# Layer 1 of a two-layer hybrid block: adaLN dots taken out of the input projection, a retention norm set behind two attention heads, and every move between partitions on the gpsimd queue

## The chip, the cores and the metric

One core of one Trainium2 chip runs the whole program. The metric is device time of one launch in microseconds (us), as the median of several runs. Below, PE is the matrix engine (TensorE), DVE the vector engine, ACT the scalar engine, POOL the gpsimd engine, and SP the sync engine, which does nothing here but issue DMAs. Each engine takes its instructions one after another in the order in which the program was written to its queue, and waits at an instruction until the data it needs is there.

## What is computed

Two layers, each with a token mix and an MLP, over 512 latent tokens and 256 context tokens of width 1024. The parts that matter here are cut from the reference:

```python
mod_x = (jax.nn.silu(c) @ w_ada[l] + b_ada[l])[:, None, :]       # 6 x 1024 numbers per layer
sh1, sc1, g1, sh2, sc2, g2 = jnp.split(mod_x, 6, axis=-1)
hx = modulate(rmsnorm(x, norm_mix[l]), sh1, sc1)
...
rq_l, rk_l, rv_l, rg_l, cq_l, ckv_l, kpe_l, u_l = split_proj(hx @ w_in)
...
ret_l = retention_out(o_rl, rg_l)          # 4 retention heads, head norm, gate
mla_l = blocked_attend(qn_l, qp_l, kn_all, kpe_all, v_all)      # 8 heads of 96
pool_l = pool_branch(u_l, w_pool, pool_scale)
out_l = jnp.concatenate([ret_l, mla_l, pool_l], axis=-1) @ w_out
x = x + g1 * ox
x = x + g2 * sq_relu_mlp(modulate(rmsnorm(x, norm_mlp[l]), sh2, sc2), w_ff1[l], w_ff2[l])
```

Twelve pieces of 512 numbers make up the adaLN vector of a layer. The first four (shift and scale of the mix) are needed at the layer's start; pieces 4 and 5 (g1) at the end of its token mix, 6 to 9 (shift and scale of the MLP) after it, 10 and 11 (g2) inside the MLP.

## The kernel before, in words

All activations stand transposed, features on partitions and tokens along the free axis. Every fp32 matmul is done as three fp32r matmuls (`mm3`), a high and a low part of each operand. So each weight tile that DMA brings into a buffer `raw` is split: ACT copies the high part (line 228) and DVE subtracts to get the low part (line 237), both into a tile `wt`. Weight and row loads are all issued by SP (line 253).

**adaLN as dots.** For layer 1 the adaLN vector isn't computed by matmuls but on DVE: one *dot* loads a 128x512 piece of `w_adaT` (256 KB) into a buffer `rows`, of which there are three (`N_RR`), and one `scalar_tensor_tensor` with an accumulating output (line 492) multiplies it by the broadcast silu(c) and sums. Eight dots make one of the twelve pieces, followed by two small adds (lines 499 and 500). A buffer is loaded again only when its dot has been done.

**Tasks, streams and the order on the queues.** The program is a list of tasks with costs. `merge` interleaves several lists in proportion to their costs. `layer_mix` builds the token mix of a layer as: rk and rq (retention keys and queries) first; then a merge of the values `rv_tok` and the other input projections with the dots of the key "in"; then a merge of the two retention pairs (`ret_pair`, ordered by `lagged`) with q, k and v of the first heads and the dots of "ret"; then eight attention heads in two halves, `att[0:4]` merged with the dots of "att" and `att[4:8]` with those of "att2". After that comes the MLP, whose first up projections are merged with the dots of "ff1". Which pieces belong to which key stands in the table `where` in `build`; those named in none are done in the MLP of layer 0. The framework then settles the final order of each engine's queue from these tasks, and it may place an instruction that is free early ahead of others; the order on the queues, not that of the list, is what the engines follow.

**Names.** `rv` is the result of `rv_tok` for one of six tiles of 128 tokens, in one of four PSUM buffers; ACT copies 32 columns of it out (`kp`, line 753), DVE takes the head means (`mu`, lines 756 and 757) and writes `V` (line 758), which releases the PSUM buffer. So the fifth tile, rv4, can begin only when V of rv0 has been written, and rv5 when V of rv1 has. `A` is the result of a projection: u0, u1 (pooling), ckv, cq0, cq1. `sc` are attention scores, DVE takes their row maximum (`st`, line 1033), ACT exponentiates (`p`, line 1034), PE transposes (`pT`) and multiplies with v (`pv`, `po`).

**Moves between partitions.** Head and rope parts of q and k have to change partition, which a DMA from SBUF to SBUF does (`move`, line 234). Layer 1 has 64 of them: 16 for `KS`, 16 for `QQ` and 8 for each of four pairs of heads (`q<-rope`, `q<-q`, `k<-k`, `k<-kpT`). A counter sends them to gpsimd and SP in turn, 32 each (`MV`, line 74).

Of the kernel before, what the change touches and what calls it, by code (L numbers as in the profile page):

```python
# [73 lines left out]
MV = lambda k, i: (i + 1) % 2  # L74
# [70 lines left out]
def merge(*streams):  # L145

    total = [max(sum(t.cost for t in s), 1e-9) for s in streams]
    done = [0.0] * len(streams)
    at = [0] * len(streams)
    out = []  # L150
    while True:
        live = [i for i in range(len(streams)) if at[i] < len(streams[i])]
        if not live:
            return out
        i = min(live, key=lambda j: (done[j] + 0.5 * streams[j][at[j]].cost) / total[j])
        t = streams[i][at[i]]
        at[i] += 1
        done[i] += t.cost
        out.append(t)


class Net:
# [67 lines left out]
    def move(self, out, src, kind):  # L230

        self.nm_ = getattr(self, "nm_", 0) + 1
        q = MV(kind, self.nm_)
        (self.nc.gpsimd, self.nc.sync, self.nc.scalar)[q].dma_start(out.bitcast(F32), src.bitcast(F32))

    def lo(self, out, src, hi):
# [440 lines left out]
    def layer_mix(self, l, late):  # L677
# [111 lines left out]
        def sig(i):  # L789
                t, e = self.tmp("sig")[:, :qw], self.tmp("sig")[:, :qw]  # L790
                nc.vector.tensor_scalar(t, s["rg"][:, i, :qw], -40.0, None, op0=ALU.max)
                nc.scalar.activation(e, t, AF.Exp, scale=-1.0)
                nc.scalar.activation(t, e, AF.Ln, bias=self.one)
                nc.scalar.activation(e, t, AF.Exp, scale=-1.0)
                nc.vector.tensor_tensor(s["rg"][:, i, :qw], s["rg"][:, i, :qw], e, op=ALU.mult)
# [188 lines left out]
        def q_pair(p):  # L984
            u, off = 1 + p // 2, 256 * (p % 2)
            t = s["q", 2 * p] = self.d("q")
            for o, n in qg:
                ps = self.B([P, n], "q")
                self.lin1(ps, mu[u], CQ, 2, o, n, woff=off)
                self.hi(t[:, 0, o:o + n], ps, scale=QK_SCALE)  # L990
                nc.vector.scalar_tensor_tensor(t[:, 1, o:o + n], ps, QK_SCALE, t[:, 0, o:o + n].bitcast(F32),
                                               op0=ALU.mult, op1=ALU.subtract)
            q = s["q", 2 * p + 1] = self.d("q")
            self.move(q[0:64, :, :qw], t[64:128, :, :qw], "q")
            for h in (2 * p + 1, 2 * p):
                for j in range(2):
                    self.move(s["q", h][64 + 16 * j:80 + 16 * j, :, :qw], s["qr"][j][16 * h:16 * h + 16, :, :qw], "qr")

        def k_pair(p):
            t = s["k", 2 * p] = self.d("k")  # L1000
            for o, n in ALL:
                ps = self.B([P, n], "k")
                self.lin1(ps, mu[1], CKV, 1, o, n, woff=512 + P * p)
                self.hi(t[:, 0, o:o + n], ps)
                self.lo(t[:, 1, o:o + n], ps, t[:, 0, o:o + n])
            k = s["k", 2 * p + 1] = self.d("k")
            self.move(k[0:64], t[64:128], "k")
            self.move(k[64:96], s["kpT"][0:32], "kr")
            self.move(t[64:96], s["kpT"][0:32], "kr")

        def v_quad(g, tk):
            ps = self.B([P, 256], "v")
            w = mu[2]
            x = CKV(0)[:, :, tk * P:(tk + 1) * P]
            c = slice(512 + 256 * g, 768 + 256 * g)
            self.mm3(ps, x[:, 0], x[:, 1], w[:, 0, c], w[:, 1, c], True, True)
            if tk == 0:
                s["v", g] = self.d("v", F32, (P, NT, 4, 64))
            nc.scalar.activation(s["v", g][:, tk], ps.rearrange("p (h e) -> p h e", h=4), AF.Copy)
# [184 lines left out]
        else:  # L1204
            early, mid, late = self.early
# [5 lines left out]
            early = [t for e in early for t in (behind[1], e, behind[0])]  # L1211
# [14 lines left out]
        if not l:  # L1226
# [12 lines left out]
        kv = lambda p: [Task(qc, lambda: q_pair(p), (mu[1 + p // 2],)),  # L1239
                        Task(kc, lambda: k_pair(p), (mu[1],))]  # L1240
        vq = lambda g: [Task(330, lambda tk=tk: v_quad(g, tk), (mu[2],)) for tk in range(NT)]
# [4 lines left out]
            J[n] = keys[2 + i]  # L1246
        j = lambda names: [J[n] for n in names.split()]
        ex = [self.extra.pop((n, l), []) for n in ("in", "ret", "att", "att2")]
        def lagged(n, sg):
            r = sum(ret, [])  # L1250
            i = len(ret[0]) - 1
            fin = r.pop(i)
            i = min(i + n, len(r) - 1)
            r.insert(i, fin)
            r.insert(max(len(r) - 1 - sg, 0), Task(0, lambda: sig(1)))
            r.insert(min(sg, i), Task(0, lambda: sig(0)))
            return r

        po, uq = pre[:2], pre[2:3]
        out = first[:n_first] + merge(first[n_first:] + (j('u1 u0 F KX ckv cq0 kn E cq1 rg0 SX qn K0 K1 SL ST rg1 uq') if l == 0 else j('u0 u1 ckv kpe KX cq0 kn cq1 F rg0 qn E SX K0 K1 SL ST rg1')), ex[0]) + merge(lagged(LG[l], SG[l]), (po + kv(0) + vq(0) if l == 0 else uq + kv(0) + vq(0)), ex[1])  # L1260
        att = att_tasks()
        sp = [Task(0, lambda n=n, i=i, at=at: mix_split(n, i, at)) for n, at in (("ret", 0), ("pool", 6)) for i in range(2)]
        early = sp + [Task(self.lin_cost(4, qg), lambda m=m: out_early(m), (out_units[m // 2],)) for m in range(NK)]
        out += (merge(merge(sum(att[0:2], []), kv(1) + vq(1)) + merge(sum(att[2:4], []), kv(2) + kv(3)), ex[2]) + merge(sum(att[4:8], [])[:-1], early, ex[3]) + att[7][-1:] if l == 0 else merge(merge(sum(att[0:2], []), kv(1) + po[:1] + vq(1) + po[1:] + kv(2)) + merge(sum(att[2:4], []), kv(3)), ex[2]) + merge(sum(att[4:8], [])[:-1], early, ex[3]) + att[7][-1:])
        out.append(Task(0, lambda: self.psum(0, 8)))
        return out

# [333 lines left out]
    def build(self):  # L1601
        nc, a = self.nc, self.a
        self.extra = {}
        self.gated = []
        self.mark = None
        tasks, late = [], []
        self.setup()
        LC = [(0, NL, 0), (NL, NC, 1)]

        def start(i):  # L1610
            if i == 0:
                self.stat_start()
            for k in (2 * i, 2 * i + 1):
                self.stat_push(k, 0, T)

        def begin():
            self.ahead, self.after = True, self.rows

        self.x_tiles(T)
        for i in range(4):  # L1620
            nc.sync.dma_start(self.x[i], a["xT"][:, 2 * i:2 * i + 2, :])
        first = [Task(0, lambda i=i: start(i)) for i in range(4)]
        ada = [self.ada_tasks(0, (n,), True) for n in range(4)]
        nl, ncx = self.norm_tasks(0, self.G1, 0, LC)
        zipped = sum(([a, b] for a, b in zip(first, ada[2])), [])
        tasks += first + nl[:2] + ncx[:1] + ada[2] + ada[0] + [Task(0, begin)]
        self.early = (ada[1] + ada[3], nl[2:6] + ncx[1:5], nl[6:] + ncx[5:])
        where = [dict(inv=(10,), att=(4,), ret=(5, 7), att2v=(6, 8, 9), ff1v=()),
                 dict(inv=(4,), attv=(5, 6), att2v=(7, 8, 9), ff1v=(10, 11))]
        for i in range(DEPTH):  # L1630
            for nme, cs in where[i].items():
                rows = nme[-1] == "v"
                ts = (self.ada_rows_tasks if rows else self.ada_tasks)(i, cs)
                key = nme[:-1] if rows else nme, i
                self.extra[key] = merge(self.extra.get(key, []), ts)
        rest = [n for n in range(12) if n not in sum(where[1].values(), ())]
        self.extra["ff", 0] = self.ada_rows_tasks(1, rest)
        gate = self.ada_rows_tasks(0, (11,))
        self.extra["out", 0] = merge(self.extra.get(("out", 0), []), gate[:4])
        self.extra["ff1", 0] = merge(self.extra.get(("ff1", 0), []), gate[4:])  # L1640
        sr = [Task(0, self.silu_rows), Task(0, self.decays)]
        self.sr = sr
        for l in range(DEPTH):
            tasks += self.extra.pop(("pre", l), [])
            tasks += self.layer_mix(l, late)
            out, late, whole, groups = self.layer_out(l)
            tasks += merge(out, self.extra.pop(("out", l), []))
            ff, late = self.layer_ff(l, whole, groups, late)
            tasks += ff

        self.emit(tasks + late)
        self.ps.close()
# [121 lines left out]
```

## Time and profile before

| | |
|---|---|
| median of 3 runs | 1567.8 us (1564.02 to 1570.93) |
| the profiled execution | 1565.01 us, of which the span of the profile is 1562.9 us |
| mean granted clock of PE | 0.992 of full speed |
| busy share of the span | PE 96%, DVE 76%, ACT 51%, POOL 2% |

The span is the time from the first to the last instruction of one execution, and about 2 us lie around it. Times within the profile are microseconds from the start of that span. Layer 0 fills the first 900 us of it. The token mix of layer 1 begins at about 909 us, its last input projections at 968 us, its attention at about 1050 us, and the MLP of layer 1 at 1205 us.

### The profile page before, as it was taken

How to read it: one execution, taken by the hardware profiler on the slowest of the kernel's cores; microseconds unless marked ns; L12 is line 12 of the kernel's file. 1: busy time of each engine (PE TensorE's matmuls, PEld its weight loads, DVE VectorE, ACT ScalarE, POOL GpSimd, SP SyncE). 2: the span in 40 equal slices, each digit the busy share in tenths (PEclk: the TensorE clock that was granted, in tenths of full speed). 3: DMA queues.
4: the chain of work that ended last, by engine and by line, in shares of the span. 5: the costliest groups of instructions: out<-in, count | busy, mean ns of one | idle time of the engine just before them, and what ended most of it. 6: DMA issues, size and time to landing. Idle time of an engine off the chain costs nothing.

```text
span 1562.9 us, 24541 instructions
## 1 busy us (share of the span) xinstructions
PE 1506.0 (96%) x9120; PEld 1329.2 (85%) x9120; DVE 1190.1 (76%) x2633; ACT 797.0 (51%) x1635; POOL 37.9 (2%) x78
## 2 busy tenths in 40 slices
PE   5999999999999999999999999989999999999997
PEld 2798667888899999999999998757888898989886
DVE  6668765887997887878869696997647895968844
ACT  4425467653654344344443463566655655455443
POOL 0110001000000000000000002001000000000000
PEclk9999999999999999999999999999999999999999
DMA  9463454555132413322223227547433443242321
GB/s 359 136 186 101 133 137 95 173 180 187 48 108 89 129 49 106 100 68 90 75 75 114 81 96 230 177 125 189 152 97 113 155 120 97 82 127 72 126 81 54
DMA packets 68903, 191.98 MB, mean 123 GB/s; under 512 B 8752, under 2 KB 11312, under 8 KB 68784
## 3 DMA queue, kind: packets, MB, share of 16 engines
q1 hardware_dynamic: 65440, 180.18, 36.6%
q0 software_dynamic: 2816, 9.70, 2.7%
q8 instruction: 72, 1.18, 0.3%
q10 hardware_dynamic: 528, 0.52, 0.1%
q14 instruction: 47, 0.39, 0.1%
HBM read 159.97 MB, written 10.49 MB: 109 GB/s over the span
## 4 chain that ended last, share of the span: by engine, by line
PE 83%; DVE 9%; ACT 3%; DMA 3%; issue 1%; SPq 0%; DVEq 0%; ACTq 0%
PE f L220 49%; PE A L220 9%; PE sc L220 4%; PE oe L220 3%; PE res L220 3%; PE pv L220 3%; PE rv L220 2%; PE pT L1052 2%; DMA rows<-w_adaT 2%; PE ada L220 1%; DVE wt L237 1%; DVE hn L572 1%; DVE h L576 1%; DVE rows L492 1%; PE ro L220 1%
## 5 line engine op out<-in xcount | busy, mean ns | idle before, releaser
L220 PE MATMUL f<-h,wt 128*128 128x384 f32 (+2 forms) x2400 | 454.3, 351 | 4.2 <-ACT h L575 3.5
L220 PEld LDWEIGHTS f<-h,wt 128*128 128x128 f32 x2400 | 416.8, 189 | 38.6 <-ACT h L575 4.5
L220 PE MATMUL f<-act,wt 128*128 128x256 f32 (+2 forms) x2664 | 410.0, 315 | 1.0 <-ACT wt L228 0.7
L220 PEld LDWEIGHTS f<-act,wt 128*128 128x128 f32 x2664 | 394.0, 188 | 15.7 <-ACT wt L228 3.5
L237 DVE TENSOR_TENSOR wt<-raw,wt 128x512 fp32r<-128x512 f32 x326 | 222.6, 687 | 101.2 <-ACT wt L228 99.9
L228 ACT ACTIVATE wt<-raw 128x512 fp32r<-128x512 f32 x326 | 198.7, 626 | 166.9 <-PE f L220 67.4
L220 PE MATMUL A<-h,wt 128*128 128x512 f32 (+1 forms) x912 | 172.9, 347 | 3.4 <-ACT h L575 2.4
L220 PEld LDWEIGHTS A<-h,wt 128*128 128x128 f32 x912 | 142.8, 190 | 29.5 <-ACT h L575 3.1
L228 ACT ACTIVATE wt<-sum 128x512 fp32r<-128x512 f32 x104 | 62.7, 629 | 126.8 <-DVE sum L264 103.4
L1437 ACT ACTIVATE b<-f 128x384 f32<-128x384 f32 (+3 forms) x100 | 50.6, 510 | 139.4 <-PE f L220 139.2
L492 DVE SCALAR_TENSOR_TENSOR rows<-rows,sbc 128x512 f32<-128x512 f32 x136 | 92.0, 685 | 8.1 <-DMA rows<-w_adaT 7.5
L220 PE MATMUL sc<-k,q 96*128 96x512 f32 (+1 forms) x384 | 87.2, 356 | 8.4 <-ACT p L1034 7.4
L220 PEld LDWEIGHTS sc<-k,q 96*128 96x128 f32 x384 | 64.4, 193 | 26.3 <-ACT p L1034 10.3
L237 DVE TENSOR_TENSOR wt<-sum,wt 128x512 fp32r<-128x512 f32 x104 | 70.3, 686 | 8.3 <-ACT wt L228 7.0
L1033 DVE TENSOR_REDUCE st<-sc 128x1 f32<-128x768 f32 x64 | 60.8, 952 | 13.7 <-PE sc L220 13.1
L1481 DVE SCALAR_TENSOR_TENSOR x<-f,mod,x 128x256 f32<-128x256 f32 (+2 forms) x148 | 69.6, 502 | 0.5 <-ACT V L1489 0.4
L1053 ACT ACTIVATE pT<-pT 128x384 f32<-128x384 f32 x128 | 56.8, 492 | 23.5 <-PE pT L1052 22.8
L228 ACT ACTIVATE act<-T 128x384 fp32r<-128x384 f32 (+1 forms) x104 | 47.3, 473 | 40.5 <-DVE T L1392 28.0
L1391 DVE TENSOR_TENSOR V<-V,f 128x384 f32<-128x384 f32 (+1 forms) x136 | 66.2, 513 | 0.1
L1034 ACT ACTIVATE p<-sc,st 128x768 f32<-128x768 f32 x64 | 57.9, 905 | 14.5 <-DVE st L1033 13.4
L220 PE MATMUL oe<-mix,wt 128*128 128x512 f32 (+1 forms) x288 | 60.8, 363 | 0.0
L237 DVE TENSOR_TENSOR act<-b,act 128x384 fp32r<-128x384 f32 (+2 forms) x94 | 47.4, 514 | 16.9 <-ACT act L228 16.9
(244 smaller groups left out, 1837.9 us busy)
## 6 DMA issues: line engine op xcount, KB each, us to landing
raw<-w_ff SPq DMA_DIRECT2D x128, 512.0 KB, 3.7
rows<-w_adaT SPq DMA_DIRECT2D x136, 256.0 KB, 3.2
raw<-w_in SPq DMA_DIRECT2D x22, 512.0 KB, 4.2
raw<-w_ada SPq DMA_DIRECT2D x16, 512.0 KB, 10.1
raw<-w_out SPq DMA_DIRECT2D x16, 512.0 KB, 4.2
rows<-w_ada SPq DMA_DIRECT2D x24, 256.0 KB, 3.1
x<-xd SPq DMA_DIRECT2D x6, 768.0 KB, 8.1
x<-xT SPq DMA_DIRECT2D x4, 768.0 KB, 6.5
```

The source lines that it names most:

```text
L220: return self.nc.tensor.matmul(out, l, r, start=start, stop=stop)
L228: self.nc.scalar.activation(out, src, AF.Copy, **k)
L237: return self.nc.vector.tensor_tensor(out, src, hi.bitcast(F32), op=ALU.subtract)
L492: nc.vector.scalar_tensor_tensor(out, w, 1.0, self.sbc[:, v, half], op0=ALU.mult, op1=ALU.mult, accum_out=acc[:, v, i, j:j + 1])
L572: nc.vector.scalar_tensor_tensor(t[:, :n], self.X(k)[:, o:o + n], G, self.ss[:, 1, o:o + n], op0=ALU.mult, op1=ALU.mult)
L1033: nc.vector.tensor_reduce(st[:, 0:1], ps, axis=AX, op=ALU.max, negate=True)
L1034: nc.scalar.activation(p, ps, AF.Exp, bias=st[:, 0:1], accum_out=st[:, 1:2])
L1052: nc.tensor.transpose(ps[:, kt, :], p[:, (k0 + kt) * P:(k0 + kt + 1) * P], self.ident)
L1053: nc.scalar.activation(s["pT", h, qt // 2][:, k0:k0 + 3, c], ps, AF.Copy)
L1391: add = lambda x, y, z, op=ALU.add: nc.vector.tensor_tensor(x, y, z, op=op)
L1437: nc.scalar.activation(b[:, at:at + n], ps, AF.Relu)
L1481: self.mark = nc.vector.scalar_tensor_tensor(x, ps[:, at - o:at - o + n], g[:, cond:cond + 1], x, op0=ALU.mult, op1=ALU.add)
```

## The change

Three things change, all for layer 1 alone.

1. `move` sends every move of layer 1 to gpsimd (queue 0) instead of alternately to gpsimd and SP.
2. The last two tasks of the second retention pair (the sigmoid of the gate, `sig(1)`, and the norm `fin_b`) are taken out of the retention stage, kept in `held`, and merged with the attention heads 2 and 3. The dots of "att" are merged with this second part only, heads 0 and 1 run without, and q and k of the third pair move to the first part.
3. Piece 4 moves from "in" to "att", piece 6 from "att" to "att2": "in" gets no dots (8 before), "att" 16 as before, "att2" 32 (24 before). The total remains.

```diff
@@ move
-        q = MV(kind, self.nm_)
+        q = 0 if self.layer else MV(kind, self.nm_)
@@ layer_mix
+        held = []
         def lagged(n, sg):
...
-            r.insert(max(len(r) - 1 - sg, 0), Task(0, lambda: sig(1)))
+            if l:
+                held.extend([Task(0, lambda: sig(1)), r.pop()])
+            else:
+                r.insert(max(len(r) - 1 - sg, 0), Task(0, lambda: sig(1)))
...
-   merge(merge(sum(att[0:2], []), kv(1) + po[:1] + vq(1) + po[1:] + kv(2)) + merge(sum(att[2:4], []), kv(3)), ex[2]) + ...
+   merge(sum(att[0:2], []), kv(1) + po[:1] + vq(1) + po[1:] + kv(2)) + merge(merge(sum(att[2:4], []), held + kv(3)), ex[2]) + ...
@@ build
-                 dict(inv=(4,), attv=(5, 6), att2v=(7, 8, 9), ff1v=(10, 11))]
+                 dict(attv=(4, 5), att2v=(6, 7, 8, 9), ff1v=(10, 11))]
...
+            tasks.append(Task(0, lambda l=l: setattr(self, "layer", l)))
```

What this does to the queues is seen only in the order of the instructions. The first difference on DVE is at the values rv of layer 1. In the kernel before, DVE's queue has there, after the third dot of layer 1, the means and V of one rv tile after another, and no dot until all six are done:

```order
L756 TENSOR_REDUCE mu_9949<-rv_9921 128x4
L757 TENSOR_SCALAR mu_9949<-mu_9949 128x4
L237 TENSOR_TENSOR rope_9883<-rm_9878,rope_9883 128x512
L756 TENSOR_REDUCE mu_9983<-rv_9957 128x4
L757 TENSOR_SCALAR mu_9983<-mu_9983 128x4
L758 TENSOR_TENSOR V_9946<-rv_9921,mu_9949 128x256
L758 TENSOR_TENSOR V_9946<-rv_9957,mu_9983 128x256
```

In the changed kernel 24 dots stand between the mean of rv0 and V of rv0. This is the beginning of that stretch, on DVE's queue again (`rows_…` is the buffer load of one dot):

```order
L756 TENSOR_REDUCE mu_9945<-rv_9917 128x4
L492 SCALAR_TENSOR_TENSOR rows_11153,acc_11151<-rows_11153,sbc 128x512
L237 TENSOR_TENSOR rope_9871<-rm_9866,rope_9871 128x512
L237 TENSOR_TENSOR rope_9879<-rm_9874,rope_9879 128x512
L757 TENSOR_SCALAR mu_9945<-mu_9945 128x4
L492 SCALAR_TENSOR_TENSOR rows_11180,acc_11151<-rows_11180,sbc 128x512
L756 TENSOR_REDUCE mu_9975<-rv_9949 128x4
L492 SCALAR_TENSOR_TENSOR rows_11183,acc_11151<-rows_11183,sbc 128x512
L757 TENSOR_SCALAR mu_9975<-mu_9975 128x4
L492 SCALAR_TENSOR_TENSOR rows_11208,acc_11151<-rows_11208,sbc 128x512
```

And this is its end, still on DVE's queue, with the first two V; the low half of u1's first weight (`wt_10099`) stands behind the fourteenth dot of the layer, and five more dots stand between V of rv1 and V of rv4:

```order
L492 SCALAR_TENSOR_TENSOR rows_11656,acc_11686<-rows_11656,sbc 128x512
L492 SCALAR_TENSOR_TENSOR rows_11661,acc_11686<-rows_11661,sbc 128x512
L758 TENSOR_TENSOR V_9942<-rv_9917,mu_9945 128x256
L758 TENSOR_TENSOR V_9942<-rv_9949,mu_9975 128x256
L756 TENSOR_REDUCE mu_10005<-rv_9979 128x4
```

Counted over DVE's queue, the 48 dots of pieces 4 to 9 stand as follows in the changed kernel: 3 ahead of the means of rv, 24 between the mean and V of rv0, 5 from there to V of rv4, 16 from there to the first row maximum of the attention (line 1033), and none inside the attention. In the kernel before: 3 ahead of the means, none among rv, 23 from there to the first row maximum, and 22 inside the attention. The 16 dots of pieces 10 and 11 in the MLP stay where they were.

On SP's queue the moves `KS` and `QQ` stood between the weights of the input projection in the kernel before:

```order
L253 DMA raw_9804<-w_in 128x1024
L234 DMA KS_9776<-rope_9771 32x768 x4
L234 DMA KS_9777<-rope_9771 32x768 x4
L253 DMA raw_9836<-w_in 128x1024
L253 DMA raw_9841<-w_in 128x1024
L234 DMA QQ_9886<-rope_9883 32x2x512 x2
L234 DMA QQ_9887<-rope_9883 32x2x512 x2
```

In the changed kernel the same stretch of SP's queue holds loads alone, and of the 17 from the fifth of these on 16 are loads of rows:

```order
L253 DMA raw_9800<-w_in 128x1024
L253 DMA raw_9832<-w_in 128x1024
L253 DMA raw_9837<-w_in 128x1024
L253 DMA raw_9915<-w_in 128x1024
L253 DMA rows_11153<-w_adaT 128x512
L253 DMA rows_11180<-w_adaT 128x512
L253 DMA rows_11183<-w_adaT 128x512
L253 DMA raw_10105<-w_in 128x1024
```

On PE's queue the kernel before turns after the first nine matmuls of u0 (`A_10128`) to rv4 (`rv_10050`), then does rv5, the rest of u0, u1 and ckv:

```order
L220 MATMUL A_10128<-h_1608_9316,wt_9913 128x512 x3
L220 MATMUL A_10128<-h_1609_9317,wt_9913 128x512 x3
L220 MATMUL A_10128<-h_1610_9318,wt_9913 128x512 x3
L220 MATMUL rv_10050<-wt_9796,h_1608_9316 128x288 x3
L220 MATMUL rv_10050<-wt_9796,h_1609_9317 128x288 x3
```

In the changed kernel PE does u0 and u1 whole after rv3, 24 matmuls each; here is the end of u1 (`A_10164`) and the beginning of rv4 (`rv_10039`), and behind rv5 follows ckv:

```order
L220 MATMUL A_10164<-h_1613_9321,wt_10102 128x512 x3
L220 MATMUL A_10164<-h_1614_9322,wt_10102 128x512 x3
L220 MATMUL A_10164<-h_1615_9323,wt_10102 128x512 x3
L220 MATMUL rv_10039<-wt_9792,h_1608_9316 128x288 x3
L220 MATMUL rv_10039<-wt_9792,h_1609_9317 128x288 x3
```

So rv4, which waits for V of rv0, has moved behind u1 on PE, and V of rv0 has moved behind 24 dots on DVE. On POOL's queue the 16 moves of `KS` and the 16 of `QQ` now stand in a row, and behind them the 32 moves of the pairs of heads.

## Rows read from the trace of the kernel before

**Rows 1.** The page, parts 1 and 4: busy shares, and the chain that ended last by engine.

```profile
PE 1506.0 (96%) x9120; PEld 1329.2 (85%) x9120; DVE 1190.1 (76%) x2633; ACT 797.0 (51%) x1635; POOL 37.9 (2%) x78
...
PE 83%; DVE 9%; ACT 3%; DMA 3%; issue 1%; SPq 0%; DVEq 0%; ACTq 0%
```

**Rows 2.** Windows: us, busy of PE, PEld, DVE, ACT, POOL, PEclk, DMA, GB/s.

```profile
1040.00:1080.00 40.00, 35.09 (x202) 27.73 (x200) 33.26 (x81) 27.50 (x62) 3.20 (x6) 0.91 0.65 183
1080.00:1120.00 40.00, 37.01 (x238) 29.66 (x237) 29.24 (x72) 26.97 (x61) 2.62 (x5) 0.96 0.66 173
```

**Rows 3.** Waits of PE, 940 to 1110 us: total us, times, longest.

```profile
PE sc L220 <- ACT p L1034: 6.3, 2, 3.3
PE ro L220 <- DVE P L882: 2.4, 1, 2.4
PE sc L220 <- issue: 1.1, 1, 1.1
```

**Rows 4.** Windows around the two falls of PE's clock; columns as in rows 2.

```profile
1053.60:1060.50 6.90, 5.55 (x20) 4.98 (x21) 6.25 (x15) 4.47 (x10) 0.69 (x2) 0.51 0.66 151
...
1094.60:1098.10 3.50, 3.50 (x15) 3.21 (x14) 2.53 (x9) 2.88 (x7) 0.51 (x1) 0.51 0.58 151
```

**Rows 5.** Chain that ended last, 1077 to 1095 us: start, length, what.

```profile
1084.56 6.13 DMA rows<-w_adaT
...
1093.49 1.38 PE sc L220 x6
```

**Rows 6.** SP's timeline: start, length with the waits inside, what it issues.

```profile
953.27 7.10 SPq L234 DMA_DIRECT2D QQ<-rope  x8
...
1083.08 1.39 SPq L234 DMA_DIRECT2D q<-rope  x1
```

**Rows 7.** POOL's timeline, its half of the moves QQ.

```profile
951.85 4.22 POOL L234 DMA_DIRECT2D QQ<-rope  x8 [2.09 <-DVE rm L667]
```

**Rows 8.** DMA issues, 940 to 1000 us: queue, count, KB each, median us to landing.

```profile
QQ<-rope POOLq DMA_DIRECT2D x8, 128.0 KB, 4.5
QQ<-rope SPq DMA_DIRECT2D x8, 128.0 KB, 4.7
```

**Rows 9.** Tile rows, 940 to 1110 us: duration ns min/median/max, and landing.

```profile
L492 DVE SCALAR_TENSOR_TENSOR rows<-rows,sbc x47: 672/685/694, 944.3 to 1109.1; 128x512 f32<-128x512 f32 x47
...
DMA to landing us min/median/max: 2.6/3.6/6.1
```

**Rows 10.** Timeline of PE from rv0 on.

```profile
947.52 12.95 PE L220 MATMUL rv<-wt,h 128*128 128x288 f32 x96 [0.69 <-ACT rq L740]
960.31 2.27 PE L220 MATMUL A<-h,wt 128*128 128x512 f32 x9
962.41 6.50 PE L220 MATMUL rv<-wt,h 128*128 128x288 f32 x48
968.75 18.95 PE L220 MATMUL A<-h,wt 128*128 128x512 f32 x92
```

**Rows 11.** Timeline of DVE, 951 to 970 us.

```profile
951.72 0.42 DVE L756 TENSOR_REDUCE mu<-rv 128x4 f32<-128x256 f32 x1
...
954.93 0.75 DVE L758 TENSOR_TENSOR V<-rv,mu 128x256 f32<-128x256 f32 x2
...
969.44 0.42 DVE L756 TENSOR_REDUCE mu<-rv 128x4 f32<-128x256 f32 x1
```

**Rows 12.** Windows of DVE alone: us, DVE busy, PEclk, DMA share, GB/s.

```profile
947.00:969.50 22.50, 12.06 (x28) 1.00 0.77 228
969.50:1053.00 83.50, 77.11 (x189) 1.00 0.53 160
1053.00:1104.00 51.00, 38.70 (x97) 0.90 0.74 193
```

**Rows 13.** The same windows, line 492 alone; two records for each dot.

```profile
969.50:1053.00 83.50, 15.62 (x46) 1.00 0.53 160
1053.00:1104.00 51.00, 13.62 (x40) 0.90 0.74 193
```

More of the change, by code (lines that the diff above doesn't have):

```diff
@@ L1263, in layer_mix @@
         early = sp + [Task(self.lin_cost(4, qg), lambda m=m: out_early(m), (out_units[m // 2],)) for m in range(NK)]
-        out += (merge(merge(sum(att[0:2], []), kv(1) + vq(1)) + merge(sum(att[2:4], []), kv(2) + kv(3)), ex[2]) + merge(sum(att[4:8], [])[:-1], early, ex[3]) + att[7][-1:] if l == 0 else merge(merge(sum(att[0:2], []), kv(1) + po[:1] + vq(1) + po[1:] + kv(2)) + merge(sum(att[2:4], []), kv(3)), ex[2]) + merge(sum(att[4:8], [])[:-1], early, ex[3]) + att[7][-1:])
+        out += (merge(merge(sum(att[0:2], []), kv(1) + vq(1)) + merge(sum(att[2:4], []), kv(2) + kv(3)), ex[2]) + merge(sum(att[4:8], [])[:-1], early, ex[3]) + att[7][-1:] if l == 0 else merge(sum(att[0:2], []), kv(1) + po[:1] + vq(1) + po[1:] + kv(2)) + merge(merge(sum(att[2:4], []), held + kv(3)), ex[2]) + merge(sum(att[4:8], [])[:-1], early, ex[3]) + att[7][-1:])
         out.append(Task(0, lambda: self.psum(0, 8)))
@@ L1605, in build @@
         self.mark = None
+        self.layer = 0
         tasks, late = [], []
```

## The prediction

> **What bounds the kernel now.** I read the page first. PE is busy for 96% of the span and makes up 83% of the chain that ended last; DVE is 9% of it and DMA 3% [rows 1]. So a gain or a loss is PE time that stands idle or runs at a lower clock, and the next view to read is where that happens in layer 1. The windows of 40 us show it: of the 80 us from 1040 on, PE is busy for 35.09 + 37.01, which leaves 7.9 idle, and the granted clock is 0.91 and 0.96 there [rows 2]. The waits say what ended the idle time: 6.3 us in two waits of scores on ACT's `p`, 3.3 the longest, so the other is 3.0 [rows 3]. Behind each PE runs at half its clock (0.51, the lower of its two levels) for 6.9 and 3.5 us [rows 4]; with 5.55 and 3.50 us of work at that rate, 49% of it, 2.7 and 1.7 us, is lost. The attention thus has 6.3 + 4.4 = 10.7 us in these two places that a change of order could win.
>
> What is behind the second place is read from the chain: the scores at 1093.49 follow a load of rows issued at 1084.56 that took 6.13 us to land [rows 5]. DVE was at a dot, in order, with the row maximum of the scores behind it. SP's timeline shows why the load was issued late: SP stood at a move from 1083.08 to 1084.47 [rows 6].
>
> The stage before it has little to win. In the 83.5 us between the last mean of rv and the first row maximum DVE is busy for 77.11 [rows 12], 15.62 of it with 23 dots (46 records, two a dot) [rows 13]. DVE leads there, PE follows.
>
> **The change, part by part.** *Moves on gpsimd.* SP's eight `QQ` end at 953.27 + 7.10 = 960.4 [rows 6]; POOL's eight take 4.22 from 951.85, 0.53 each [rows 7]. Sixteen on POOL take 8.4 and end at 960.3, as SP's did. They land as late from either queue, 4.5 and 4.7 us [rows 8]. I cost this at nothing: the first users of either come after PE's ckv, at 987.7 (968.75 + 18.95) [rows 10], so 20 us of projections hide it. Without that cover it would cost what POOL issues behind SP's old end, less than 1 us. For SP it means that it can issue loads of rows from about 945 on instead of 960.4. That is what lets the dots come early.
>
> *24 dots ahead of V of rv0.* This is the term that decides. The order has only a few weight halves and means among them, so DVE goes at the pace at which rows arrive. A dot takes 0.69, a load lands after 3.6 (2.6 to 6.1) [rows 9], and a buffer is loaded again only after its dot. A buffer's round is thus 3.6 + 0.69 = 4.3 us, and with three buffers a dot comes every 1.43 us. The bounds: at the fastest landing 1.10; at one halfway between median and slowest, 4.9, 1.86. I take the median; at 0.77 the DMA engines are busier in this stage than after it [rows 12], but many of the loads there are weights that come anyway.
>
> The first mean ends at 951.72 + 0.42 = 952.1 [rows 11]. Three dots have their rows by then; with two rope halves (0.69 each) and the mean of rv1 they end at about 956. 21 more take 21 x 1.43 = 30, so V of rv0 is written at 986.4 instead of 955.3 [rows 11]; by the bounds at 979 and 995.
>
> *PE behind it.* rv0 to rv3 end at 947.52 + 12.95 = 960.5, nine matmuls of a projection take 2.27, so 24 take 6.05 and u0 ends at 966.5 [rows 10]. u1's first low half stands behind 8 of the 21 dots, at 956 + 11.4 + 0.7 = 968.2: PE waits 1.7 and ends u1 at about 974.5. Then it waits for V of rv0, 12 us. rv4 and rv5 take 6.50 and end at 992.9. After an idle stretch of 3 us the clock fell and cost 2.7 and 1.7 [rows 4]; after 12 us I add 2.5: 995.4. Before, the same work (rv0 to rv5, u0, u1) was done at 968.75 + 39 x 0.25 = 978.5 [rows 10]. PE is 17 us late.
>
> *What is recovered up to the attention.* DVE takes the mean of rv5 at 995.5 instead of 969.44 [rows 11], 26 us late, but has less to do: 16 dots instead of 23, 7 x 0.68 = 4.8 [rows 13], and two weight halves of cq0 that it has done while waiting, 1.4. That leaves 70.9 of 77.1 busy. Of the 6.4 idle [rows 12] I keep half, since PE and ACT, only 17 late, are ahead of it now. 995.5 + 70.9 + 3.2 = 1069.6 for the first row maximum, which stood at 1053.0: 16.6 late. For PE alone it would be 995.4 plus the 73 us that it needed before, 1068.5, nearly the same.
>
> *What the attention gives back.* DVE is busy for 38.70 of 51 us there, 13.62 with 20 dots [rows 12, 13]; none is left. The second wait can't recur: 3.0, and the half clock behind it, 1.7. The first (3.3 and 2.7) is the start of the attention and depends on what else DVE holds: I take half, 3.0. Together 7.7. The norm of the second pair moves into heads 2 and 3; its PE work is the same, and its DVE work lies in the 26 us that DVE then has free (51 - 38.70 + 13.62): nothing. Without that room its two matmuls and some six DVE operations would stand in a head's way, about 0.7 us each at the dot's size, 4 in all. The bounds of this part are 4.7 and 10.7.
>
> *Sum.* 16.6 - 7.7 = +8.9. Against the profiled execution's 1565.0 that is 1573.9; the median of the runs is 2.8 higher, which would give 1576.7. I take **1575**. The likeliest case alone reaches from 1569 to 1582: about 6 either way, from 1.2 to 1.7 us for a dot.
>
> **The rivals.**
>
> *Slow rows (chance 0.16).* `QQ`, weights and rows want the same DMA engines at once; at 1.86 us for a dot V comes at 995, another 9 us late: 1584. For it: 6.1 us landings do occur [rows 9]. Against: only beside moves of the attention, as far as the chain shows.
>
> *No change (0.20).* Rows land in 2.6, V comes at 979, PE is done with rv5 near 988 and 9.5 late; the first row maximum comes at 1062, 9 late, and 7.7 are given back: 1567. For it: SP has nothing to issue but loads. Against: with three loads in flight the median is 3.6.
>
> *Faster (0.13).* PE, not DVE, sets the stretch after rv. V comes at 979 and PE is 9.5 late at rv5; then, with seven dots fewer on DVE, PE's waits on `P` (2.4) and ahead of the first scores (1.1) go [rows 3], and the scores begin 6 late. The attention gives back all 10.7 and the 1.6 of idle time there that are not waits on `p` (7.9 - 6.3) [rows 2, 3]; the last retention matmuls, taken into heads 2 and 3, fill PE where it would wait for an exponential, another 1 to 3. 6 - 12.3 - 2 = -8: 1559. It decides if a dot comes in under 1.15 us and DVE is never late behind rv5. Against: in before PE had to wait for DVE here, not the other way.
>
> *Late moves (0.06).* With all eight moves of a pair of heads on POOL, issued at 0.53 each, the last goes out 2.1 us later than with four on each queue; if the first scores of pairs wait for it, twice on the path, 3 to 4 us more: 1579. The Trainium skill, "DMA: Bandwidth & Descriptors", section "SWDGE vs HWDGE vs iDMA", has gpsimd write its descriptors through SBUF, where DVE can lock it out, while SP's are immune. No row here shows it: POOL's `QQ` went out at their pace with DVE busy for 12.06 of 22.5 us [rows 7, 12].
>
> **How the numbers follow.** The forecast has 0.45. A measurement can't tell less than 0.5%, 7.8 us, from no change: slower begins at 1575.6, faster at 1560. The forecast's own range lies across the first of these; I give 0.25 of its chance to slower and 0.20 to same. Slower: 0.25 + 0.16 + 0.06 = 0.47. Same: 0.20 + 0.20 = 0.40. Faster: 0.13. The range goes from 1561, which leaves the faster case out, to 1588, past the slow one at 1584.
>
> **What would show it.** Right, if after the mean of rv0 DVE alternates between waits on rows and dots for some 30 us, with V of rv0 near 986; if PE has one idle stretch of about 12 us behind u1, ended by V (line 758), with a fall of its clock after it; if the first row maximum comes near 1070; and if no dot and no wait on rows stands in the attention. Wrong at the pace of rows, if V comes before 980; wrong at the recovery, if PE is busy without a gap from rv4 to the first scores and these come before 1060; wrong at the attention, if PE still waits for `p` twice for 3 us.

## The result

The changed kernel takes 1589.1 us (median of 4 runs, 1583.7 to 1595.4) against 1565.9 for the kernel before in the same measurement. The medians differ by 23 us; the ratio of all runs is 1.0138, 95% interval 1.0112 to 1.0164, which is 22 us. The forecast was +8.9 us, at 1575, with a range up to 1588, so the result lies 1 us beyond the range. The sign was right, the size some 2.5 times too small.

The profiled execution of the changed kernel has a span of 1581.8 us, 18.9 longer than that of before. Layer 0, which the change doesn't touch, differs by a few us from one execution to the next: the first matmul of rv comes between 946 and 956 us in all the executions looked at here. So below every place in layer 1 is given as time after the first matmul of rv ("after rv0 begins"). By that clock the changed kernel is 22.3 us late at the first matmul of the MLP, which agrees with the medians.

| us after rv0 begins | before | changed | forecast |
|---|---|---|---|
| V of rv0 written from | 7.4 | 50.2 | 38.9 |
| rv5 and u1 both done on PE | 30.5 | 59.6 | 47.9 |
| first row maximum of the attention | 105.4 | 131.6 | 122.1 |
| first matmul of the MLP | 249.2 | 271.5 | 258 |

The waits of PE in the changed kernel, 940 to 1110 us (total us, times, longest), stand against [rows 3]:

```profile
PE A L220 <- DVE wt L237: 12.5, 1, 12.5
PE rv L220 <- DVE V L758: 12.1, 1, 12.1
PE sc L220 <- ACT p L1034: 3.3, 3, 1.2
PE ro L220 <- DVE P L882: 2.3, 2, 1.4
PE sc L220 <- DMA k<-kpT: 1.6, 1, 1.6
```

Two waits on DVE are new, 24.6 us together, where there was none. PE's timeline shows where they are; the rows answer to [rows 10]:

```profile
946.07 12.96 PE L220 MATMUL rv<-wt,h 128*128 128x288 f32 x96 [0.69 <-ACT rq L740]
958.87 6.25 PE L220 MATMUL A<-h,wt 128*128 128x512 f32 x26
977.65 7.09 PE L220 MATMUL A<-h,wt 128*128 128x512 f32 x22 [12.54 <-DVE wt L237]
996.83 8.86 PE L220 MATMUL rv<-wt,h 128*128 128x288 f32 x48 [12.08 <-DVE V L758]
```

After rv0 to rv3 and u0 PE waits for the low half of u1's first weight, and after u1 for V of rv0. The same work also takes longer: rv4 and rv5 8.86 instead of 6.50. The granted clock there is the lower of the two levels, from these windows of PE alone (us, PE busy, PEclk, DMA share, GB/s):

```profile
968.00:977.70 9.70, 0.04 (x1) 0.50 0.80 199
977.70:981.00 3.30, 3.30 (x8) 0.50 0.67 228
981.00:984.70 3.70, 3.70 (x16) 0.94 0.86 271
984.70:997.00 12.30, 0.22 (x2) 0.64 0.69 229
997.00:1001.00 4.00, 4.00 (x17) 0.50 0.72 244
```

It fell in the idle stretches, and 3.3 and 4.0 us of PE's work ran at the lower level behind them; half of that is lost, 1.7 and 2.0. The windows at 0.94 and 0.91 behind these add 0.7. In all, rv0 to rv5, u0 and u1 keep PE busy for 35.0 us instead of 30.5. This shows in three windows of PE (columns as above; x counts the matmuls). The first runs from rv0 until rv5 and u1 are done, the second to the first row maximum, the third to the MLP. Before the change:

```profile
947.50:978.00 30.50, 30.48 (x193) 1.00 0.76 238
978.00:1052.92 74.92, 68.85 (x398) 1.00 0.50 148
1052.92:1196.70 143.78, 137.46 (x869) 0.96 0.50 146
```

and in the changed kernel:

```profile
946.07:1005.70 59.63, 35.00 (x193) 0.77 0.84 238
1005.70:1077.67 71.97, 67.76 (x390) 0.98 0.50 145
1077.67:1217.57 139.90, 135.52 (x878) 1.00 0.37 105
```

What DVE does meanwhile is read from its timeline; a few of its rows between the first mean and V, which answer to [rows 11]:

```profile
954.04 0.69 DVE L492 SCALAR_TENSOR_TENSOR rows<-rows,sbc 128x512 f32<-128x512 f32 x1 [3.79 <-DMA rows<-w_adaT]
...
968.44 0.69 DVE L492 SCALAR_TENSOR_TENSOR rows<-rows,sbc 128x512 f32<-128x512 f32 x1 [2.99 <-DMA rows<-w_adaT]
...
976.91 0.69 DVE L237 TENSOR_TENSOR wt<-raw,wt 128x512 fp32r<-128x512 f32 x1
...
996.27 0.75 DVE L758 TENSOR_TENSOR V<-rv,mu 128x256 f32<-128x256 f32 x2
```

Dot after dot, each behind a wait on its rows, and the weight half that PE wants in their middle. The sixth dot of the layer ends at 957.6, the 27th at 996.3: 21 dots in 38.8 us, 1.85 each. Of these the first eight, up to the weight half, take 2.4 each, the thirteen behind it 1.5. How rows land in that stretch differs between its two parts. For 943 to 976 us the view of the tile `rows` gives:

```profile
DMA to landing us min/median/max: 3.7/6.8/10.8
```

and for 976 to 998 us:

```profile
DMA to landing us min/median/max: 2.6/3.4/4.4
```

The border is where the moves end. In windows of 4 us (us, PEclk, DMA share, GB/s) the DMA share stands above 1 from 944 to 972, so the engines are to be read as full. They move 236 to 296 GB/s there; the kernel before moves 228 at a share of 0.77 in the same stage [rows 12]:

```profile
944.00:948.00 4.00, 1.00 1.03 286
...
960.00:964.00 4.00, 1.00 1.06 244
...
972.00:976.00 4.00, 0.50 0.83 232
976.00:980.00 4.00, 0.50 0.51 167
```

POOL issues moves of KS and QQ until 968.3 (the last five take 2.67 us from 965.62 on). That is 22.2 us after rv0 begins, where 12.8 was forecast. The moves of QQ begin 5.6 us later than before, as the two rope halves that they carry stand behind the fourth dot on DVE, and between moves POOL waits for earlier ones to land. In the DMA issues of 944 to 970 us rows and moves are late alike:

```profile
rows<-w_adaT SPq DMA_DIRECT2D x9, 256.0 KB, 6.8
QQ<-rope POOLq DMA_DIRECT2D x16, 128.0 KB, 7.3
KS<-rope POOLq DMA_DIRECT2D x10, 96.0 KB, 7.3
```

So what [rows 8] showed at 4.5 us takes 7.3 here, in company.

### The profile page after: what moved, and what is told of

The parts are those of the page before. It is cut to its first block, busy times and chain, and to the rows that moved or that the text cites. A ratio compares the mean times of both kernels' runs of the same rounds, so it can differ in the third digit from the quotient of the medians.

```text
span 1581.8 us, 24532 instructions
## 1 busy us (share of the span) xinstructions
PE 1503.7 (95%) x9120; PEld 1326.0 (84%) x9120; DVE 1190.5 (75%) x2633; ACT 795.0 (50%) x1635; POOL 54.3 (3%) x110
## 5 line engine op out<-in xcount | busy, mean ns | idle before, releaser
L220 PE MATMUL A<-h,wt 128*128 128x512 f32 (+1 forms) x912 | 174.6, 349 | 16.4 <-DVE wt L237 12.5
L220 PE MATMUL res<-mix,wt 128*128 128x256 f32 (+1 forms) x384 | 58.2, 311 | 1.9 <-DVE om L1073 1.9
## 6 DMA issues: line engine op xcount, KB each, us to landing
raw<-w_ada SPq DMA_DIRECT2D x16, 512.0 KB, 10.2
```

The lines of the kernel that those rows point to most:

```text
L220: return self.nc.tensor.matmul(out, l, r, start=start, stop=stop)
```

## The experiments

The theory from here on: the place of the 24 dots ahead of V of rv0, on an engine that takes its work in order, is what costs the time, and the full DMA engines set its price. Rivals: the moves cost by being on one queue; or the later dots and the norm cost. The order of the instructions told ahead of the runs which part of the change moves the dots: the queue of KS and QQ alone. With them on both queues no dot stands ahead of V, whatever else is changed.

**The queue alone** (`e1_moves_only`): the kernel before, with

```diff
-        q = MV(kind, self.nm_)
+        q = 0 if self.layer else MV(kind, self.nm_)
```

> Only the queue of the moves is changed; table of dots and place of the norm are those of before. DVE's queue has 24 dots ahead of V of rv0, as in the changed kernel. Theory (the dots ahead of V cost the time): 1583 to 1595 us, V of rv0 at 990 or later, PE waits on DVE in the input stage of 20 us or more. Rival (later dots and the norm behind two heads cost it): 1563 to 1570, as before.

1595.9 us, ratio 1.0196 (1.0167 to 1.0225). V of rv0 comes 50.0 us after rv0 begins, and the two waits of PE are 12.0 each. The queue alone makes the whole loss and more; the rest of the change takes some of it back, 4 us by the place of the MLP's first matmul (275.9 against 271.5) and 6 by the medians against the kernel before.

**All but the queue** (`e2_moves_on_both`): the changed kernel with that line undone.

> The changed kernel with the moves alternating between gpsimd and SP again. No dot stands ahead of V of rv0. Theory (the dots ahead of V cost the time): 1558 to 1568, V of rv0 near 955. Rival (later dots and the norm behind two heads cost it): 1580 or more.

1562.8 us, ratio 0.9979 (0.9958 to 1.0000). V of rv0 at 7.4 us, as before the change. The rival that the later dots and the norm cost falls.

**The pairs' moves alone on gpsimd** (`e7_pair_moves_gpsimd`): the changed kernel with

```diff
-        q = 0 if self.layer else MV(kind, self.nm_)
+        q = 0 if self.layer and kind not in "KQ" else MV(kind, self.nm_)
```

> The changed kernel with the 32 moves of KS and QQ alternating again; the 32 moves of the pairs of heads stay on gpsimd. No dot stands ahead of V of rv0. Theory (the dots ahead of V): 1558 to 1568. Rival (moves on one queue cost by being late, in the attention): about half of the loss stays, 1572 to 1580, with waits of scores on k<-kpT of over 1 us a pair.

1571.4 us, ratio 1.0022 (1.0004 to 1.0040). V of rv0 at 7.4 us, so the great loss is gone, but the time is outside the theory's range and 8.5 us above the run before. The views of `rows` from 1040 to 1100 us differ. With the pairs' moves on gpsimd:

```profile
L492 DVE SCALAR_TENSOR_TENSOR rows<-rows,sbc x30: 667/685/693, 1043.1 to 1098.9; 128x512 f32<-128x512 f32 x30
...
  DMA rows<-w_adaT: 9.1, 11
```

and with all moves on both queues:

```profile
L492 DVE SCALAR_TENSOR_TENSOR rows<-rows,sbc x20: 671/684/693, 1047.4 to 1097.1; 128x512 f32<-128x512 f32 x20
...
  DMA rows<-w_adaT: 0.6, 1
```

30 dots instead of 20 stand around the start of the attention, and DVE waits 9.1 us for rows there instead of 0.6. The waits of scores on `p` that stand behind this are 10.2 us instead of 5.1. Whether the moves themselves cost anything this run doesn't tell, so the next was made.

**KS and QQ alone on gpsimd** (`e8_ks_qq_gpsimd`): as above with `kind in "KQ"`.

> The changed kernel, but only the moves of KS and QQ are all on gpsimd; the 32 moves of the pairs of heads alternate again. 24 dots stand ahead of V of rv0. Theory (the moves of the pairs on one queue take back part of what the attention gives, as the run with these alone on gpsimd was 8 us slower than the one with none): the wait of scores on k<-kpT goes, 3 to 8 us less than the changed kernel, 1581 to 1586. Rival (that difference came from where the dots stood in the attention, and here none stand there): within 2 us of the changed kernel, 1587 to 1591.

1589.4 us, ratio 1.0135 (1.0116 to 1.0154): the same as the changed kernel, so the rival of this run holds. The wait on k<-kpT is gone, and nothing is won by it. The pairs' moves on one queue cost nothing that shows here, where no dot stands in the attention. That the 8.5 us of the run before came from the place of the dots is thus the likely reading; no run holds the dots in place there. With e1 and e2 the great loss lies with KS and QQ.

**Dots after V** (`g1_dots_after_v`): the changed kernel, all moves on gpsimd, and in `rv_tok`

```diff
-            nc.vector.tensor_tensor(s["V"][:, tk], rv, mu_..., op=ALU.subtract)
+            v = nc.vector.tensor_tensor(s["V"][:, tk], rv, mu_..., op=ALU.subtract)
+            if l and tk == NT - 1:
+                self.mark = v
```

where every dot of layer 1 is issued after `self.mark`.

> The changed kernel, all moves on gpsimd, with every dot of the token mix of layer 1 ordered after V of rv5. Theory (the dots ahead of V cost the time by DVE's order): 1558 to 1570, V of rv0 near 955, no idle stretch of PE over 3 us in the input stage. Rival (16 KS and 16 QQ moves on one queue fill the DMA engines, and the weights come late whatever DVE does): weights of u1 and ckv land 5 us late or more, 1575 or more.

1574.3 us, ratio 1.0044 (1.0027 to 1.0061): 15 of the 22 us are won back by order alone, with every move still on gpsimd. PE has no long idle stretch in the input stage:

```profile
960.07 11.40 PE L220 MATMUL A<-h,wt 128*128 128x512 f32 x48
973.35 6.59 PE L220 MATMUL rv<-wt,h 128*128 128x288 f32 x48 [1.87 <-DVE V L758]
```

The range was missed by 4 us and V came at 25.5 us, not near 7.4: four weight halves now stand ahead of it on DVE, each behind a wait for ACT. PE did u0 and u1 meanwhile and was 2 us late at rv5 and u1 (32.6). The first row maximum comes at 104.8 us. The rest, 5 us in this execution and 7 by the ratio, is lost behind that, in the attention, where DVE waits 11.4 us for rows (1040 to 1120 us).

**The dots held in place, with short moves** (`f_short_moves`): 24 dots are held ahead of V of rv0, 11 of them ahead of u1's first weight half as in the changed kernel, and the moves of KS and QQ carry a few columns. `rv_sub` is the write of V, taken out of `rv_tok`; `self.dot` is the last dot.

```diff
+            rvs = rvs[:2] + dots[:27] + [Task(0, lambda tk=tk: rv_sub(tk, *s.pop(("rv", tk)))) for tk in range(2)] + rvs[2:]
...
+            with self.tc.issue_after(self.dot.ins) if l and tk < 2 else nullcontext():
...
+        if self.layer and kind == "K":
+            out, src = out[:, 0:64], src[:, 0:64]
+        if self.layer and kind == "Q":
+            out, src = out[:, :, 0:32], src[:, :, 0:32]
```

> The changed kernel with 24 dots held ahead of V of rv0 as there, but each move of KS carries 64 columns of 768 and each of QQ 32 of 512 (the rest of these tiles is zeros), so 0.25 MB instead of 3.6; the retention is not computed by it. Theory (the moves and the rows fill the DMA engines together, and that made a dot take 1.85 us): rows land in 3 to 4.5 us, a dot every 1.3 to 1.5, V of rv0 38 to 41 us after the first matmul of rv instead of 50, and 8 to 14 us less than the changed kernel, 1575 to 1581. Rival (three buffers and the weights set the pace, whatever is moved): landings of 6 us and more as before, V at 48 or later, within 4 us of the changed kernel.

1574.3 us, ratio 1.0062 (1.0040 to 1.0083), 15 us less than the changed kernel. From 945 to 988 us rows land as the theory had it:

```profile
DMA to landing us min/median/max: 2.6/3.3/6.1
```

V of rv0 comes at 41.0 us instead of 50.2. By an estimate it would have come up to 3.6 earlier: DVE stood that long beside the memsets with which this kernel fills the tiles (last section). So with the dots at the same places, what the moves carry is worth 9 to 13 us of V. The 15 us hold one thing more: PE's order isn't that of the changed kernel. 81 matmuls of projections instead of 22 stand between u1's first weight and rv4 here, and PE does them while it would wait.

**The dots held in place, with moves on both queues** (`f_moves_on_both`): as above with whole moves, `q = MV(kind, self.nm_)`.

> 24 dots held ahead of V of rv0, but the moves alternate between gpsimd and SP as before the change. Theory (it is the place of the dots on DVE's queue that costs): V of rv0 is late by 30 us or more here too, as rows wait for SP behind the moves and land among them; 1582 to 1596. Rival (one gpsimd queue for the moves is what made rows slow): V 30 to 40 us after the first matmul of rv, 1572 to 1580.

1587.5 us, ratio 1.0134 (1.0114 to 1.0154). V of rv0 at 60.0 us; one wait of PE makes up for the two:

```profile
PE rv L220 <- DVE V L765: 21.7, 1, 21.7
```

Rows are issued from 960.8 us on here, behind the moves on SP, and DVE takes the first of the 24 dots at 972.7, 25.5 us after rv0 begins, behind four weight halves and the first operations of the pooling. PE's order differs too: 120 matmuls of projections stand ahead of rv4. From there on the dots run with no move beside them (SP's last goes out by 960.2). The view of the tile `rows` from 955 to 1008 us:

```profile
L492 DVE SCALAR_TENSOR_TENSOR rows<-rows,sbc x24: 681/691/693, 972.7 to 1006.6; 128x512 f32<-128x512 f32 x24
...
DMA to landing us min/median/max: 2.6/3.5/5.6
```

That is a dot every 1.47 us, the pace that was forecast, and no longer 1.85. Dots ahead of V thus cost as much in all with the moves on both queues as with them on one, by a late start and not by a slow pace. A single gpsimd queue isn't needed for the loss.

**The norm behind the heads** (`e4_norm_behind_heads`): the whole second part of the change, with the old table and both queues.

> Only the second part of the change: the norm of the second pair in heads 2 and 3 and the dots of att merged with these; table and queue of the moves as before. Theory: a little faster than before, by 2 to 4 us, since this and the table are all that differ from before where the moves are on both queues (0.9979 measured for both). Rival (the table gives that): as before within 1 us.

1561.9 us, ratio 0.9975 (0.9963 to 0.9988): faster than before, by 3.5 us. Of all runs it has the lowest ratio, though not one that can be told from the 0.9979 of e2. Its first row maximum comes at 101.4 us instead of 105.4, and the MLP begins 3.9 earlier. PE's waits from 900 to 1260 us are shorter than [rows 3] at both places:

```profile
PE sc L220 <- ACT p L1034: 4.7, 3, 2.5
...
PE ro L220 <- DVE P L882: 1.7, 2, 0.9
```

**The table alone** (`e3_table_only`): `dict(attv=(4, 5), att2v=(6, 7, 8, 9), ff1v=(10, 11))` in the kernel before.

> Only the table of the dots is changed. Theory (the norm behind the heads alone made the gain of the run with both, 0.9975 against 0.9979): as before, ratio 0.998 to 1.002. Rival (later dots give by themselves what the norm gives): 0.995 to 0.998.

1568.0 us, ratio 1.0000 (0.9987 to 1.0014): no difference. The second part of the change makes the gain of the two. It holds three steps (the norm itself, the dots of "att" with heads 2 and 3 only, q and k of the third pair earlier), and no run takes these apart.

**Dots kept in the attention** (`g2_dots_in_attention`): both queues, new table, held norm, and each dot after the row maximum ahead of it in the program:

```diff
-            nc.vector.tensor_reduce(st[:, 0:1], ps, axis=AX, op=ALU.max, negate=True)
+            r = nc.vector.tensor_reduce(st[:, 0:1], ps, axis=AX, op=ALU.max, negate=True)
+            if l:
+                self.mark = r
```

> Moves on both queues, new table and held norm, and each dot of the token mix of layer 1 is ordered after the row maximum that precedes it in the program, so that none can be placed in the input or retention stage. Theory (dots cost where DVE leads, and nothing where it has room): the first row maximum 10 to 15 us earlier after the first matmul of rv than before the change, part of it lost to dots in heads 2 to 7; 1555 to 1562. Rival (PE is full there anyway, and dots in the attention delay row maxima): 1563 to 1572.

1564.7 us, ratio 0.9995 (0.9979 to 1.0010). The first row maximum comes 101.1 us after rv0 begins, 4.3 earlier than before and not 10 to 15, no earlier than in e4 (101.4) or in e2 (99.8), which differs from this run by the added order alone. 48 dots taken out of DVE's way there won nothing, and PE is busy for 68.0 of the 70.6 us from the end of rv5 and u1 to the first row maximum. So PE sets that stretch, as the rival has it, and the attention with 48 dots in it is longer: 148.8 us from the first row maximum to the MLP, against 143.9 in e4 and 147.2 in e2.

## Why the prediction was right in sign and wrong in size

*The mechanism held.* Dots ahead of V of rv0, PE idle behind u1, ended by V, a fall of the clock after it, DVE alternating between waits and dots: all as forecast, with the lateness carried on to the attention. Only the idle stretch ahead of u1, forecast at 1.7 us, became as long as that behind it. By e1, e2 and g1 it is shown that this is the loss, and by f_moves_on_both that dots ahead of V cost as much when both queues move the data. With KS and QQ on gpsimd the order has the dots there (e1, e8), with these on both queues it hasn't (e2, e7); that SP's freed queue is the reason is argued from the order on SP and not tested by itself.

*The step that failed: "a load lands after 3.6 ... I take the median".* The pace of 1.43 us for a dot was made from a median over 940 to 1110 us, which holds the quiet parts too. Measured: 1.85, with landings of 6.8 in the first part of the stretch and 3.4 after it. What was overlooked stands in one sentence. The moves were costed "at nothing" on the grounds of POOL's issue times and of when their users come; that their 3.6 MB take the same DMA engines as the rows now issued beside them was put off with "many of the loads there are weights that come anyway", though the DMA share stood at 0.77 already [rows 12] with no dot in that stretch. f_short_moves shows this to be the cause: rows land in 3.3 when the moves carry little; and in f_moves_on_both, where the dots come when the moves are done, the pace is 1.47. V came 11.3 us later than forecast: 3 from the first three rows, which landed after some 10.5 us and not in time, and 8.8 from the pace of the 21 dots (the forecast's own sum, 956 + 30, is 986.0 and not 986.4).

The trace of before held a better number. The loads of rows that it issues in this very stage, six from 961 to 985 us, take longer than the median of the long stretch:

```profile
DMA to landing us min/median/max: 3.1/5.0/5.5
```

At 5.0 the prediction's own formula gives (5.0 + 0.69) / 3 = 1.90 us a dot, close to the 1.85 measured.

The rival "slow rows" had this case: V at 995, 47.5 us after rv0 begins, by 1.86 us a dot, against 50.2 and 1.85 measured, and 1584 us in all against 1589.1. It was given 0.16, on the grounds that slow landings occur only beside moves of the attention; the moves of KS and QQ were in the way for the same reason.

*What follows from it on PE.* PE was forecast 17 us late at rv5 and u1 and was 29.1 (59.6 - 30.5). The 12 us of waiting for V came as forecast, 12.1; the wait for u1's weight was 12.5 instead of 1.7, because the eight dots ahead of it are those that waited longest; the lower clock cost 4.5 instead of 2.5. These three are the whole: 12.1 + 12.5 + 4.5 = 29.1.

*Recovery up to the attention, and what the attention gives back.* 0.4 and 7.7 were forecast, 2.9 and 3.9 came (29.1 late at rv5 and u1, 26.2 at the first row maximum, 22.3 at the MLP). The split between the two can't be compared: by the windows above, PE does 8 matmuls fewer than before up to the first row maximum (390 instead of 398) and 9 more after it (878 instead of 869). Together it is 8.1 forecast and 6.8 measured. In these two windows PE is idle for 8.6 us instead of 12.4 and busy for 203.3 instead of 206.3. The second wait did go, and both falls of the clock in the attention: the waits on `p` are 3.3 instead of 6.3, and the granted clock is 1.00 in every window from 1064 to 1217. What the forecast did not have is a fall of the clock ahead of the first row maximum. Behind the two waits on `P`, 2.3 us together, it is 0.50 from 1060 to 1063 us, which costs 1.5. Before, the wait on `P` of 2.4 [rows 3] had no such fall behind it.

The sum was thus off by 12.1 (PE late) + 1.3 (recovery and attention) = 13.4: 8.9 + 13.4 = 22.3. Most of it follows from V, 11.3 us later than forecast. (The forecast's check by PE alone took 73 us up to the first row maximum; its own places, 978.5 and 1053.0, give 74.5. Nothing in the sum hangs on it.)

*Norm and table.* Both were costed at nothing. The table is (1.0000). The second part of the change, the norm with what goes with it, is worth 3.5 us by itself, which a wait of PE in [rows 3], 2.4 on `P`, had hinted at.

*The rivals not met.* "No change" and "faster" needed rows in 2.6 us. "Late moves": the wait on k<-kpT appeared, once, for 1.6 us, and e8 shows that the pairs' moves cost nothing measurable on one queue.

## What to carry to other kernels

When a change frees a queue, list what will be issued through it earlier, and add up the bytes against what already moves in that stretch: the price of a load there is the landing time under that load, not the median over a longer stretch. On an engine that works in order, work that waits on DMA may be set early only behind what another engine is waiting for; here 24 small dots ahead of a 0.4 us subtraction and among them a weight half held PE for 24.6 us. Change the queue, the table and the order one by one: of the three parts of this change, each made alone, one cost 29 us, one gave 3.5, and one did nothing.

## What the runs showed of the hardware

In the kernel with short moves a DVE operation on 4 columns took 4.35 us, and ended when POOL's memsets ended. On DVE, then on POOL:

```profile
952.95 4.35 DVE L767 TENSOR_SCALAR mu<-mu 128x4 f32<-128x4 f32 x1
...
957.39 0.17 DVE L767 TENSOR_SCALAR mu<-mu 128x4 f32<-128x4 f32 x1
```

```profile
951.90 5.37 POOL L714 MEMSET QQ<- 128x1536 f32 x4
957.20 8.43 POOL L238 DMA_DIRECT2D QQ<-rope  x16
```

The tensor_tensor and scalar_tensor_tensor operations that ran on DVE in the memsets' first microsecond, with two inputs each, kept their 0.68. The Trainium skill, "GPSIMD Engine Reference", section "Key points", says that gpsimd shares its SBUF interfaces with VectorE, and that the two contend when DVE runs in a two-port mode or reads two SBUF inputs. The 4.35 us agree with contention of the first kind, though no run shows in which mode the operation ran; the two-input operations at 0.68 show none of the second beside these memsets, which read nothing.

With moves and rows in flight together the profile's DMA share stands at 1.03 to 1.06 with 236 to 296 GB/s, and both land later: rows, which SP issues, in 6.8 us instead of the 3.4 after the moves, and moves of QQ, which POOL issues, in 7.3 instead of 4.5. The Trainium skill, "DMA: Bandwidth & Descriptors", section "Issuing engines are not separate DMA queues", has all DMAs run on the same 16 engines and interleave; the runs here agree.
